# An encoder block on one core: selection for block 1 apart from that for blocks 2 and 3, a longer lead of A over V, and all gate rows made by ACT

## The chip, the core and the metric

The kernel runs on one core of a Trainium2 chip. TensorE (PE) multiplies matrices, VectorE (DVE) and ScalarE (ACT) do element-wise work, GpSimd (POOL) does element-wise work and issues indirect DMAs, SyncE (SP) issues plain DMAs. Each engine works through its own instructions strictly in the order in which they were issued and waits on semaphores for the others; so an instruction that waits holds up all that stand behind it on its engine. DMA transfers share 16 DMA engines.

The metric is the device time of one launch in microseconds (us). Three runs of the kernel before took 3649.86, 3670.61 and 3675.56 us; the median is 3670.61 us. In this kernel a difference below about 1% (some 37 us) can't be told from no change.

## What is computed

One layer of an encoder, on 512 tokens of width 2048, in float32: RMS norm, one input projection, attention and a short convolution, their gated sum through `w_out`, then PEER, then a small gated embedding. The change lies in PEER:

```python
q = (xc @ w_q).reshape(PEER_CHUNK, PEER_HEADS, 2, PEER_HALF)      # 8 heads, two halves of 128
s = jnp.einsum('thpc,hpnc->thpn', q, sub_keys)                    # 128 keys for each half
sv, si = lax.top_k(s, 16)                                         # the best 16 of each half
cand = sv[:, :, 0, :, None] + sv[:, :, 1, None, :]                # 16 x 16 sums
tv, tpos = lax.top_k(cand, 16)                                    # the best 16 of them
gate = jax.nn.softmax(tv, axis=-1)
a = jnp.einsum('td,thkd->thk', xc, u[eidx])                       # eidx: one of 16384 experts
hid = jax.nn.gelu(a) * gate
out = jnp.einsum('thk,thkd->td', hid, v[eidx])
```

Each token thus picks 8 x 16 = 128 experts of 16384; `u` and `v` have a row of 2048 numbers for each expert.

## The kernel before

The 512 tokens are four blocks of 128. The program is written in the order in which each engine is to work (a schedule by hand): Python generators hand over after a stretch of work, and credits in nominal microseconds set how much of one strand is issued between two pieces of another. Most weights are split into a high and a low part (ACT makes the high part, DVE or POOL the low one), and a product takes three matmuls (`mm3`, lines 218 to 220).

PEER is done in two ways. For **blocks 0 and 1** the picked rows are fetched: an indirect DMA, issued by POOL (`gather`, line 390), brings one row of `u` or `v` for each of the 128 tokens, 1.05 MB, and one DVE instruction over 128x2048 uses it (line 417 for `u`, line 440 for `v`, which adds to `gp`). Each block takes 128 such steps for `u` and 128 for `v`. They are a background strand `bg`: `bg(us)`, called at many places in the program, adds credit, and a step is issued while credit is positive (a step costs 2.45 of credit). The constants that begin with BG are the credits of the places. Four buffers `rows` hold fetched rows; a gather waits on POOL until DVE has used the row before in its buffer.

For **blocks 2 and 3** (256 tokens) all 16384 experts are multiplied, in 128 chunks of 128. `A` (line 1226 and following: `split_u`, and the matmuls) makes `a = u h` for a chunk, 48 matmuls over 256 columns, with gelu on ACT at line 1368. `V` multiplies the gated result with `v`; one `v_step` is 12 matmuls over 512 columns and a sum on DVE (`add_up`, line 1279), two steps for a chunk. The gates come from a dense matrix G (token by expert), which is built from the picks: `one_hots` makes, for four tokens at a time, rows `oj` (a one where the second index is) and `oi` (the gate's value where the first index is); four matmuls multiply them (`Gp`, line 1184), ACT evicts (`Gst`, line 1185), and the result goes to DRAM. There are 64 such groups.

The order of the part that matters here:

- **The queries** (`peer_q`, called at the end with blocks 1 to 3): for each of 8 heads the query matmuls `qA` (block 1) and `qB` (blocks 2, 3) in four pieces, with `bg(BG2)` after each; then `scores` makes the scores `hp`, and `sel.head` selects the best 16 on DVE. `Sel(3)` does this for three blocks in one go. With more than one block, `head` lets ACT spread the positions into `eq` (line 567) between two pieces of DVE work.
- **A alone**: `A` for the first LA chunks, with no `V`. Beside it runs `prepare` (what is left of the selection, then the 64 groups of G), BGD of credit to each quarter of a chunk, and `bg` with BG0. For chunks 0 to LA-9 the gelu goes to DRAM (`gad`) and is fetched again later.
- **V catches up**: at chunk LA, 2 x (LA - 8) steps of `V` alone, with `bg(BGV)` after each.
- **A and V together** for the chunks LA to 127, `V` 8 chunks behind, with `bg(BGU)` four times a chunk.
- Then the last 8 chunks of `V`, what is left of `bg`, and the embedding.

In `one_hots`, the first NACT of the four `oi` rows of a group are made by ACT (Abs of the difference, then Relu), row number NACT by POOL, the others by DVE.

Of the kernel before, what the change touches and what calls it, by code (L numbers as in the profile page):

```python
# [9 lines left out]
F32 = mybir.dt.float32  # L10
# [4 lines left out]
AF = mybir.ActivationFunctionType  # L15
# [3 lines left out]
P = 128  # L19
# [15 lines left out]
PH = 8  # L35
TOPK = 16
# [7 lines left out]
WSR = 8  # L44
BGA = 1.0
BGE = 0
LA = 24
BGV = 1.5
WSP = 8
WS0 = 4  # L50
BGF = 1.6
EV0 = 2
BG0 = 1.2
BGU = 1.5
BG1 = 2.2
BG2 = 1.5
BGD = 1.7
STEP = 2.45
VB = 7
WSH = 8  # L60
LAGC = 8
AHEAD = 3
NACT = 1
NROWS = 4


# [1 line left out]
def block_kernel(ctx: ExitStack, tc: tile.TileContext, a, out):  # L68
    nc = tc.nc
    ctx.enter_context(tc.manual_schedule())  # L70

    def pool(name, bufs=1, **kw):
        return tc.tile_pool(name=name, bufs=bufs, **kw)
# [13 lines left out]
    def bank(name, group=None):  # L87

        group = group or every[0]
        i = banks_used[group] = banks_used.get(group, -1) + 1  # L90
        tag = group[i % len(group)]
        return (pp if tag in LOW else high[0]).tile([P, 512], F32, name=name, tag=tag, bufs=1)


    class Stream:
        def __init__(self):
            self.items, self.loaded, self.parts, self.halves = [], 0, [], []
            self.used, self.share, self.turn = 0, 0, 0
# [124 lines left out]
    ident = cp.tile([P, P], F32, name="ident")  # L223
# [84 lines left out]
    TB = 2 * P  # L308
    TR = S - P
    u_t, v_t = a["peer_u"][0], a["peer_v"][0]  # L310
    gd = dp.tile([16, P, P, 16], F32, name="gd")
    gad = dp.tile([LA - LAGC, P, TB], F32, name="gad")
    x1d = dp.tile([2, P, D], F32, name="x1d")
# [13 lines left out]
    def tmp(shape, dt=F32, nm="t1"):  # L327
        return lt.tile([P] + shape, dt, name=nm, tag="t1", bufs=tbufs[0])
# [185 lines left out]
    class Sel:  # L514
# [4 lines left out]

        def __init__(self, nb):  # L520
            self.nb = nb
            self.tv = lt.tile([P, nb, PH, TOPK], F32, name="tv", tag="tv")
            self.ij = [lt.tile([P, nb, P], F32, name=f"ij{s}", tag=f"ij{s}") for s in range(2)]
            self.gate = lt.tile([P, nb, P], F32, name="gate", tag="gate")

        def head(self, h, hp):
            nb, tv = self.nb, self.tv
# [49 lines left out]
        def finish(self):  # L577
# [9 lines left out]
            nc.vector.reciprocal(gs, gs)  # L587
            nc.vector.tensor_mul(gv, gv, gs[:, :, None].to_broadcast([P, nb * PH, TOPK]))

    def scores(h, psA, psB, sel, blk):  # L590
        qA = tmp([256], nm="qa")
        nc.scalar.activation(qA, psA[:, :256], AF.Copy)
        hp = lt.tile([P, sel.nb, 2, P], F32, name="hp", tag="hp", bufs=2)
        if psB:
            qB = lt.tile([P, 2, TB], F32, name="qb", tag="h2B", bufs=6)
            for s in range(2):
                nc.scalar.activation(qB[:, s, :], psB[s][:, :TB], AF.Copy)
        yield
        pt = bank("qt", ("b3",))
        for s in range(2):  # L600
            nc.tensor.transpose(pt[:, s * P:(s + 1) * P], qA[:, s * P:(s + 1) * P], ident)
        qt = tmp([256], nm="qt")
        nc.scalar.activation(qt, pt[:, :256], AF.Copy)
        if psB:
            pk = bank("ks", ("b3",))
            for b in range(2):
                for s in range(2):
                    i = b * 2 + s
                    nc.tensor.matmul(pk[:, i * P:(i + 1) * P], qB[:, s, b * P:(b + 1) * P], keysT[:, 2 * h + s, :],
                                     start=True, stop=True)  # L610
            nc.scalar.activation(hp[:, 1:].rearrange("p b s n -> p (b s n)"), pk, AF.Copy)
        yield
        pk = bank("ks", ("b3",))
        for s in range(2):
            nc.tensor.matmul(pk[:, s * P:(s + 1) * P], qt[:, s * P:(s + 1) * P], keysT[:, 2 * h + s, :],
                             start=True, stop=True)
        nc.scalar.activation(hp[:, 0].rearrange("p s n -> p (s n)"), pk[:, :256], AF.Copy)
        yield
        yield from sel.head(h, hp)
        hs = slice(h * TOPK, (h + 1) * TOPK)  # L620
        i, j = (x[:, 0, hs] for x in sel.ij)
        nc.vector.scalar_tensor_tensor(i, i, 128.0, j, op0=ALU.mult, op1=ALU.add)
        nc.vector.tensor_copy(idxA[blk][:, hs], i)
        bg.add(u_steps(blk, h))
# [38 lines left out]
    def finish_A(b, sel):  # L663
        sel.finish()
        nc.vector.tensor_copy(gateA[b], sel.gate[:, 0, :])
        bg.add(v_steps(b))
# [45 lines left out]
    with pool("p0", side="right") as p0:  # L712
# [65 lines left out]
        ps = bank("cw", LOW)  # L778
# [186 lines left out]
    lt = lta = lts.enter_context(pool("late0", side="right"))  # L965
# [14 lines left out]
    for p_ in range(8):  # L980
        r = {}
        for nm, x, kt in (("ga", h0, KC), ("gc", h0, KC), ("ya", attn0, 8), ("yc", conv0, 8)):
            ps = bank(nm)
# [27 lines left out]
    sel = Sel(1)  # L1011
# [50 lines left out]
    with pool("mix2") as m2:  # L1062
        for p_ in range(8):
            sg = {}
            for nm, xh, xl, kt in (("ga", hH, hL, KC), ("gc", hH, hL, KC), ("ya", attnH, attnL, 8),
# [11 lines left out]
                for n in range(2):  # L1077
                    ps = pss[n][:, :TR]
# [33 lines left out]
    for c in range(0, KC, 2):  # L1112
        for dst, t0 in ((mA, 0), (mB, P)):
            t = mrg[:, c:c + 2, t0:t0 + dst[0].shape[2]]
            h = dst[0][:, c:c + 2, :]
# [4 lines left out]
    lt = lts.enter_context(pool("late", side="right"))  # L1120
    nc.sync.dma_start(x1_1, xv[1])
    for b in range(2):
# [5 lines left out]
    tA, tB = tA_pair(), tB_pair()  # L1128
    rsA[1] = rs[:, 0:1]
    turn = turner([(accB[0], rs[:, 1:2], tB, 0), (accB[1], rs[:, 2:3], tB, 1), (x1_1, rs[:, 0:1], tA, 0)], gffn,  # L1130
                  lambda: lt.tile([P, 512], F32, name="h2B", tag="h2B", bufs=6))
    for q in range(1, 4):
        turn(q)
    sel = Sel(3)
    ws.share = WSH
    sel_rest = peer_q(tA, tB, sel, 1, BG2)

# [4 lines left out]
    def prepare():  # L1142
        nonlocal dn
        yield from sel_rest
        finish_A(1, sel)
        yield 3.0
        for b in range(2):
            ps = bank("pkt", ("b2",))
            for i, t in enumerate((sel.ij[0], sel.ij[1], sel.gate)):
                nc.tensor.transpose(ps[:, i * P:(i + 1) * P], t[:, 1 + b, :], ident)  # L1150
            for i in range(3):
                nc.scalar.activation(pickT[i][:, b * P:(b + 1) * P], ps[:, i * P:(i + 1) * P], AF.Copy)
        nc.scalar.mul(pickT[3], pickT[0], -1.0)
        lts.close()
        dn = dns.enter_context(pool("dense"))
        yield 1.0
        def one_hots(t0):
            oj = dn.tile([P, 4, P], F32, name="oj", tag="vraw", bufs=4)
            oi = dn.tile([P, 4, P], F32, name="oi", tag="vh" if t0 % 8 else "vl", bufs=VB)

            for i in range(NACT):
                nc.scalar.activation(oi[:, i, :], io128, AF.Abs, bias=pickT[3][:, t0 + i:t0 + i + 1])
            for i in range(NACT):
                nc.scalar.activation(oi[:, i, :], oi[:, i, :], AF.Relu, bias=pickT[2][:, t0 + i:t0 + i + 1],
                                     scale=-4.0)
            nc.vector.tensor_tensor(oj, pickT[1][:, t0:t0 + 4, None].to_broadcast([P, 4, P]),
                                    io128[:, None, :].to_broadcast([P, 4, P]), op=ALU.is_equal)
            for i in range(NACT, 4):
                t = slice(t0 + i, t0 + i + 1)
                (nc.gpsimd if i == NACT else nc.vector).tensor_scalar(  # L1170
                    oi[:, i, :], io128, pickT[0][:, t], pickT[2][:, t], op0=ALU.is_equal, op1=ALU.mult)
            return oj, oi

        nxt = [one_hots(4 * i) for i in range(3)]
        for tg in range(16):
            st = dn.tile([P, P, 16], F32, name="Gst", tag="G", bufs=2)
            for q in range(4):
                t0 = tg * 16 + q * 4
                oj, oi = nxt.pop(0)
                if t0 + 12 < TB:  # L1180
                    nxt.append(one_hots(t0 + 12))
                ps = bank("Gp", ("b2", "b3"))
                for i in range(4):
                    nc.tensor.matmul(ps[:, i * P:(i + 1) * P], oj[:, i, :], oi[:, i, :], start=True, stop=True)
                nc.scalar.activation(st[:, :, q * 4:q * 4 + 4].rearrange("p i t -> p t i"),
                                     ps.rearrange("p (t i) -> p t i", t=4), AF.Copy)
                yield 1.3
            nc.scalar.dma_start(gd[tg], st)

    dn = None  # L1190
# [31 lines left out]
    def split_u(c, q):  # L1222
# [3 lines left out]
        nc.scalar.activation(h, t, AF.Copy)  # L1226
        (nc.gpsimd if q == 3 or (c < LA and q == 1) else nc.vector).tensor_sub(l, t, h.bitcast(F32))  # L1227
        uq[c, q] = (h, l)
# [71 lines left out]
    only = [False]  # L1300
    SP = LA - LAG

# [20 lines left out]
    for c in range(NCH + LAG):  # L1323
        if c + 1 < NCH:
            load_u(c + 1)
        if c < NCH:
            pa = bank("a", ("b0", "b1"))[:, :TB]
        if c == LA - 5:
            for _ in prep:
                pass  # L1330
            for i in range(4):
                load_ga(i)
        if c == LA - 4:
            load_G(0)
        if c == LA - 3:
            load_G(1)
# [17 lines left out]
        for q in range(4):  # L1354
# [4 lines left out]
            if c < LA:  # L1359
                dve += BGD  # L1360
                while dve > 0:
                    dve -= next(prep, 100.0)
            if q % 2 == 1 and c >= LA:
                v_step(2 * (c - LAG) + q // 2)
            bg((BG0 if c < LA - 5 else BG0 / 3) if c < LA else BGU if c < NCH else BGV / 2)
        if c < NCH:
            t = ring[:, c % 9, :]
# [141 lines left out]
```

## Time and profile before

| | |
|---|---|
| median of three runs | 3670.61 us |
| the profiled execution | 3676.39 us |
| its span, first to last instruction | 3674.6 us |
| mean granted clock of TensorE | 0.959 |
| busy PE / DVE / POOL / ACT | 90% / 73% / 59% / 41% |
| DMA moved | 1131.94 MB, mean 308 GB/s |

The profile is of one execution, by the hardware. A row of the timeline has its start and length in us, the engine, the line, the operation and what it writes and reads; `x3` says that three like it follow each other, with one length for all. A row of groups has busy time, the mean of one in ns, and the idle time before them with what ended it. A row of the windows has one stretch. PE's busy time is no measure of PE at its peak, since matmuls overlap.

### The profile page before, as it was taken

Reading aid. Unit: us, or ns where it says so; the run is one execution under the profiler, and the core shown is the slowest. Engines: PE = TensorE matmul, PEld = TensorE weight load, DVE = VectorE, ACT = ScalarE, POOL = GpSimd, SP = SyncE. Lnnn points to the kernel's source line nnn. Section 1 sums busy time; section 2 is a strip of 40 time slices with the busy share of each in tenths; the row PEclk is TensorE's granted clock in tenths of the full one; section 3 lists DMA queues with packets and bytes.
Section 4 is the critical chain, followed back from the end, with each engine's and each line's share of the span. In section 5 each row is a group of like instructions: output and inputs, shape, how many; then the busy total and the mean of one; then the engine's idle time right before and its main releaser. Section 6 shows DMA issues by size and latency. Waiting matters only on the chain. (4 is left out here: it accounts for less than half of the span.)

```text
span 3674.6 us, 53569 instructions
## 1 busy us (share of the span) xinstructions
PE 3295.4 (90%) x19455; PEld 2955.6 (80%) x19455; DVE 2697.4 (73%) x3844; ACT 1507.9 (41%) x2822; POOL 2166.2 (59%) x1764
## 2 busy tenths in 40 slices
PE   7999888999999998777787898999998999899899
PEld 5999677889999977767775777888887888788687
DVE  7458688776555655999978897887887988977411
ACT  5258523343333333327743333444433443334422
POOL 2012046567888776436754676777777777776343
PEclk8999999999999999988999999999999999999899
DMA  5689778888999997548898999999999999997332
GB/s 208 219 314 339 261 274 293 295 293 337 357 356 347 366 346 269 185 162 293 314 362 317 333 380 358 396 363 392 379 361 364 378 384 384 370 374 273 126 120 81
DMA packets 265501, 1131.94 MB, mean 308 GB/s; under 512 B 25980, under 2 KB 64148, under 8 KB 195092
## 3 DMA queue, kind: packets, MB, share of 16 engines
q1 hardware_dynamic: 186324, 568.54, 43.5%
q0 software_dynamic: 74304, 541.10, 38.3%
q10 hardware_dynamic: 4608, 18.88, 1.3%
q8 instruction: 153, 2.51, 0.3%
q14 instruction: 112, 0.92, 0.1%
HBM read 1102.20 MB, written 26.21 MB: 307 GB/s over the span
## 5 line engine op out<-in xcount | busy, mean ns | idle before, releaser
L131 POOL TENSOR_TENSOR wl<-wraw,wh 128x512 fp32r<-128x512 f32 x534 | 694.7, 1308 | 544.3 <-ACT wh L129 532.5
L1213 POOL TENSOR_TENSOR vl<-vraw,vh 128x512 fp32r<-128x512 f32 x464 | 610.1, 1336 | 375.4 <-ACT vh L1212 318.0
L129 ACT ACTIVATE wh<-wraw 128x512 fp32r<-128x512 f32 x696 | 430.2, 630 | 685.1 <-PE gt L220 117.4
L440 DVE SCALAR_TENSOR_TENSOR gp<-rows,dots,gp 128x2048 f32<-128x2048 f32 x254 | 596.6, 2349 | 109.3 <-DMA rows<-in_peer_v_dram,idx 108.8
L417 DVE SCALAR_TENSOR_TENSOR rows<-rows,gp 128x2048 f32<-128x2048 f32 x256 | 581.9, 2280 | 113.5 <-DMA rows<-in_peer_u_dram,idx 113.5
L220 PE MATMUL a<-tBH,ul 128*128 128x256 f32 x2048 | 583.1, 285 | 11.4 <-DVE ul L1227 11.4
L218 PE MATMUL a<-tBH,uh 128*128 128x256 f32 x2048 | 587.0, 287 | 6.1 <-ACT uh L1226 6.1
L219 PE MATMUL a<-tBL,uh 128*128 128x256 f32 x2048 | 581.6, 284 | 0.0
L218 PE MATMUL o<-vh,hidH 128*128 128x512 f32 x1024 | 425.2, 415 | 156.2 <-DVE accB L1279 149.3
L1227 DVE TENSOR_TENSOR ul<-uraw,uh 128x512 fp32r<-128x512 f32 x360 | 415.5, 1161 | 172.5 <-ACT uh L1226 170.2
L1226 ACT ACTIVATE uh<-uraw 128x512 fp32r<-128x512 f32 x512 | 311.4, 627 | 544.0 <-PE a L219 266.4
L219 PE MATMUL o<-vl,hidH 128*128 128x512 f32 x1024 | 417.4, 408 | 3.7 <-POOL vl L1213 3.7
L220 PE MATMUL o<-vh,hidL 128*128 128x512 f32 x1024 | 415.7, 406 | 0.0
L218 PEld LDWEIGHTS a<-tBH,uh 128*128 128x128 f32 x2048 | 394.7, 193 | 15.7 <-ACT uh L1226 7.1
L220 PEld LDWEIGHTS a<-tBH,ul 128*128 128x128 f32 x2048 | 393.7, 192 | 13.3 <-DVE ul L1227 13.2
L219 PEld LDWEIGHTS a<-tBL,uh 128*128 128x128 f32 x2048 | 393.7, 192 | 8.8
L218 PEld LDWEIGHTS o<-vh,hidH 128*128 128x128 f32 x1024 | 200.3, 196 | 217.2 <-DVE accB L1279 150.9
L390 POOL DMA_INDIRECT rows<-in_peer_v_dram,idx x256 | 278.3, 1087 | 98.6 <-DVE gp L440 44.6
L1212 ACT ACTIVATE vh<-vraw 128x512 fp32r<-128x512 f32 x512 | 295.0, 617 | 90.2 <-PE o L220 87.2
L390 POOL DMA_INDIRECT rows<-in_peer_u_dram,idx x256 | 271.2, 1060 | 100.6 <-DVE rows L417 49.2
L1227 POOL TENSOR_TENSOR ul<-uraw,uh 128x512 fp32r<-128x512 f32 x152 | 201.1, 1323 | 89.8 <-ACT uh L1226 84.6
L219 PEld LDWEIGHTS o<-vl,hidH 128*128 128x128 f32 x1024 | 201.1, 196 | 46.9 <-POOL vl L1213 11.0
(388 smaller groups left out, 7103.0 us busy)
## 6 DMA issues: line engine op xcount, KB each, us to landing
uraw<-in_peer_u_cols_dram SPq DMA_DIRECT2D x256, 512.0 KB, 10.2
vraw<-in_peer_v_tiles_dram SPq DMA_DIRECT2D x256, 512.0 KB, 7.5
wraw<-in_w_in_gates_dram SPq DMA_DIRECT2D x96, 512.0 KB, 6.4
wraw<-in_w_in_conv_dram SPq DMA_DIRECT2D x64, 512.0 KB, 5.1
wraw<-in_w_out_dram SPq DMA_DIRECT2D x64, 512.0 KB, 5.6
wraw<-in_w_peer_q_dram SPq DMA_DIRECT2D x64, 512.0 KB, 4.6
wraw<-in_w_in_qkv_dram SPq DMA_DIRECT2D x40, 512.0 KB, 4.7
wring<-in_w_in_conv_dram SPq DMA_DIRECT2D x32, 512.0 KB, 4.6
```

The costliest lines, as they stand in the source:

```text
L129: nc.scalar.activation(h, t, AF.Copy)
L131: (nc.gpsimd if self.turn >= 8 else nc.vector).tensor_sub(l, t, h.bitcast(F32))
L218: nc.tensor.matmul(ps, ah, bh, start=first, stop=False)
L219: nc.tensor.matmul(ps, ah, bl, start=False, stop=False)
L220: nc.tensor.matmul(ps, al, bh, start=False, stop=last)
L390: nc.gpsimd.indirect_dma_start(out=dst, out_offset=None, in_=src, in_offset=bass.IndirectOffsetOnAxis(ap=ix, axis=0))
L417: nc.vector.scalar_tensor_tensor(t[0], t[0], 1.0, gp[0], op0=ALU.mult, op1=ALU.mult, accum_out=dots[b][:, k:k + 1])
L440: nc.vector.scalar_tensor_tensor(gp[0], t[0], dots[b][:, k:k + 1], gp[0], op0=ALU.mult, op1=ALU.add)
L1212: nc.scalar.activation(h, t[:, i, :], AF.Copy)
L1213: (nc.vector if only[0] and i else nc.gpsimd).tensor_sub(l, t[:, i, :], h.bitcast(F32))
L1226: nc.scalar.activation(h, t, AF.Copy)
L1227: (nc.gpsimd if q == 3 or (c < LA and q == 1) else nc.vector).tensor_sub(l, t, h.bitcast(F32))
```

## The change

Four things change, and the credits with them.

1. `peer_q` for blocks 1 to 3 now selects for block 1 alone (`sel = Sel(1)`). The scores of blocks 2 and 3 are kept in tiles `hpB`, one for each head, and a second object `selB = Sel(2)` selects from them in `prepare`, after the first selection has ended, beside A.
2. LA goes from 24 to 48. So A runs alone for 48 chunks, `gad` holds 40 chunks in place of 16, and V catches up with 80 steps in place of 32.
3. NACT goes from 1 to 4: ACT makes all four `oi` rows of a group, POOL and DVE none.
4. BG2 goes from 1.5 to 5.0 (queries), BG0 from 1.2 to 0.85 and BGD from 1.7 to 0.93 (A alone), and a group of G counts 0.8 in place of 1.3.

```diff
-LA = 24
+LA = 48
-BG0 = 1.2
+BG0 = 0.85
-BG2 = 1.5
-BGD = 1.7
+BG2 = 5.0
+BGD = 0.93
-NACT = 1
+NACT = 4
@@ scores
-        hp = lt.tile([P, sel.nb, 2, P], F32, name="hp", tag="hp", bufs=2)
+        hp = lt.tile([P, 1, 2, P], F32, name="hp", tag="hp", bufs=2)
         if psB:
-            qB = lt.tile([P, 2, TB], F32, name="qb", tag="h2B", bufs=6)
+            qB = lt.tile([P, 2, TB], F32, name="qb", tag="h2B", bufs=HB)
+            hpB[h] = lt.tile([P, 2, 2, P], F32, name="hpB", tag="h2B", bufs=HB)
...
-            nc.scalar.activation(hp[:, 1:].rearrange("p b s n -> p (b s n)"), pk, AF.Copy)
+            nc.scalar.activation(hpB[h].rearrange("p b s n -> p (b s n)"), pk, AF.Copy)
@@ the main stage
-    sel = Sel(3)
+    sel, selB = Sel(1), Sel(2)
@@ prepare
         yield from sel_rest
         finish_A(1, sel)
+        yield 1.5
+        for h in range(PH):
+            for _ in selB.head(h, hpB[h]):
+                yield 2.5
+        selB.finish()
         yield 3.0
         for b in range(2):
             ps = bank("pkt", ("b2",))
-            for i, t in enumerate((sel.ij[0], sel.ij[1], sel.gate)):
-                nc.tensor.transpose(ps[:, i * P:(i + 1) * P], t[:, 1 + b, :], ident)
+            for i, t in enumerate((selB.ij[0], selB.ij[1], selB.gate)):
+                nc.tensor.transpose(ps[:, i * P:(i + 1) * P], t[:, b, :], ident)
@@ one_hots
-                (nc.gpsimd if i == NACT else nc.vector).tensor_scalar(
+                nc.vector.tensor_scalar(
@@ G
-                yield 1.3
+                yield 0.8
```

How the change moves instructions can be read from the built programs. The first place is DVE in the queries, one head of the selection. Before, with `gp<-rows` a background step, the best-16 rows come by threes (three blocks):

```order
L440 SCALAR_TENSOR_TENSOR gp<-rows,dots_93,gp 128x2048
L546 TENSOR_TENSOR cand<-sv 128x3x48
L546 TENSOR_TENSOR cand<-sv 128x3x52
L549 CAST sif<-si 128x96
L504 MAX tv<-cand 128x8 x3
L506 MAX_INDEX tp<-tv,cand 128x8 x3
L508 MATCH_REPLACE z_13602<-tv,cand 128x100 x3
```

and of the change, at the same place:

```order
L440 SCALAR_TENSOR_TENSOR gp<-rows,dots_93,gp 128x2048 x2
L546 TENSOR_TENSOR cand<-sv 128x48
L546 TENSOR_TENSOR cand<-sv 128x52
L549 CAST sif<-si 128x32
L504 MAX tv<-cand 128x8
L506 MAX_INDEX tp<-tv,cand 128x8
L508 MATCH_REPLACE z_13891<-tv,cand 128x100
L510 MAX tv<-z_13891 128x8
L512 MAX_INDEX tp<-tv,z_13891 128x8
L440 SCALAR_TENSOR_TENSOR gp<-rows,dots_93,gp 128x2048 x3
```

One block in place of three is selected, and more background steps stand between. From the last `tAL` (the transposed input of the queries) to the first `ul` (A's first split on DVE) there are 65 background steps now and 20 before.

The second place is DVE beside A, in the changed program, where the low parts `ul` of A's weights (line 1235 there) now alternate with the selection from `hpB`; before, one-hot rows stood here from chunk 3 on:

```order
L440 SCALAR_TENSOR_TENSOR gp<-rows,dots_93,gp 128x2048
L1235 TENSOR_TENSOR ul<-uraw,uh 128x512
L504 MAX sv<-hpB 128x8 x2
L506 MAX_INDEX si<-sv,hpB 128x8 x2
L508 MATCH_REPLACE z<-sv,hpB 128x128 x2
L510 MAX sv<-z 128x8 x2
L512 MAX_INDEX si<-sv,z 128x8 x2
```

Counted by `ul` (two to a chunk), the selection from `hpB` lies in the chunks 3 to 29, the 64 `oj` rows in the chunks 30 to 43 (before: 3 to 14). There are 38 background steps in the chunks 0 to 29. Where A and V run together, the last background step stands in chunk 110 (before: in chunk 126), 2.45 a chunk in both programs.

The third place is ACT in the groups of G, before (`uh`: the high part of A's weights, `ring`: gelu):

```order
L1162 ACTIVATE oi<-io_86,picks 128x128
L1164 ACTIVATE oi<-oi,picks 128x128
L1185 ACTIVATE Gst<-Gp 128x4x128
L1368 ACTIVATE ring<-a 128x256
L1370 DMA gad<-ring 128x256
L1226 ACTIVATE uh<-uraw 128x512
```

and of the change:

```order
L1376 ACTIVATE ring<-a 128x256
L1378 DMA gad<-ring 128x256
L1234 ACTIVATE uh<-uraw 128x512
L1170 ACTIVATE oi<-io_86,picks 128x128 x4
L1172 ACTIVATE oi<-oi,picks 128x128 x4
L1193 ACTIVATE Gst<-Gp 128x4x128
```

A group has eight rows for `oi` on ACT in place of two.

## Rows read from the trace of the kernel before

**Rows 1.** Windows: busy us (instructions) of each engine, granted clock, DMA share, GB/s
```profile
core 0: us, PE busy (x) PEld busy (x) DVE busy (x) ACT busy (x) POOL busy (x), PEclk, DMA share, GB/s
1436.30:1638.60 202.30, 162.28 (x1264) 160.07 (x1263) 173.85 (x646) 66.06 (x123) 98.69 (x82) 0.91 0.55 185
1638.60:1693.00 54.40, 36.48 (x207) 34.59 (x207) 49.72 (x134) 25.75 (x50) 21.48 (x21) 0.68 0.53 170
1693.00:1845.00 152.00, 122.95 (x970) 117.38 (x970) 150.01 (x207) 120.77 (x226) 115.80 (x101) 0.97 0.92 336
1845.00:1921.30 76.30, 66.11 (x499) 63.58 (x498) 52.29 (x41) 31.35 (x59) 39.89 (x33) 0.94 1.01 378
1921.30:2066.00 144.70, 108.63 (x409) 82.38 (x410) 114.90 (x141) 48.18 (x95) 66.32 (x55) 0.89 0.88 317
2066.00:3388.30 1322.30, 1203.17 (x7460) 1072.21 (x7459) 1124.35 (x1099) 535.81 (x1043) 951.25 (x764) 0.97 0.96 369
3500.00:3600.00 100.00, 100.00 (x430) 80.26 (x429) 11.74 (x16) 27.60 (x45) 47.53 (x36) 1.00 0.37 116
```

**Rows 2.** Waits, 1430 to 1640: who for whom, total us, times, longest
```profile
PE ks L609 <- ACT qt L603: 39.3, 8, 10.3
ACT eq L567 <- DVE ab L558: 35.4, 7, 7.6
```

**Rows 3.** Groups of instructions on DVE in the queries, 1436.3 to 1638.6
```profile
L440 DVE SCALAR_TENSOR_TENSOR gp<-rows,dots,gp 128x2048 f32<-128x2048 f32 x20 | 46.9, 2344 | 3.3 <-DMA rows<-in_peer_v_dram,idx 3.2
L504 DVE MAX8 sv<-hp 128x8 f32<-128x128 f32 x42 | 9.4, 279 | 19.4 <-ACT hp L617 19.4
```

**Rows 4.** Timeline of DVE, block 0's selection: first instruction of two heads
```profile
452.42 0.48 DVE L504 MAX8 sv<-hp 128x8 f32<-128x128 f32 x2
460.55 0.48 DVE L504 MAX8 sv<-hp 128x8 f32<-128x128 f32 x2
```

**Rows 5.** Groups of instructions on DVE while A runs alone, 1640 to 1921
```profile
L1227 DVE TENSOR_TENSOR ul<-uraw,uh 128x512 fp32r<-128x512 f32 x47 | 41.0, 873 | 27.7 <-ACT uh L1226 27.7
```

**Rows 6.** Groups of instructions on ACT while A runs alone, 1640 to 1921
```profile
L1226 ACT ACTIVATE uh<-uraw 128x512 fp32r<-128x512 f32 x97 | 59.3, 628 | 61.5 <-DMA uraw<-in_peer_u_cols_dram 36.2 <-PE a L219 14.7 <-PE a L220 2.6
L1164 ACT ACTIVATE oi<-oi,picks 128x128 f32<-128x128 f32 x64 | 25.7, 402 | 2.1
```

**Rows 7.** Timeline of ACT beside A
```profile
1674.81 0.59 ACT L1152 ACTIVATE picks<-pkt 128x128 f32<-128x128 f32 x3
...
1709.70 0.40 ACT L1164 ACTIVATE oi<-oi,picks 128x128 f32<-128x128 f32 x1
1710.01 1.04 ACT L1185 ACTIVATE Gst<-Gp 128x512 f32<-128x512 f32 x1
1710.86 0.63 ACT L1226 ACTIVATE uh<-uraw 128x512 fp32r<-128x512 f32 x1
...
1715.15 0.41 ACT L1368 ACTIVATE ring<-a 128x256 f32<-128x256 f32 x1
1716.05 0.63 ACT L1226 ACTIVATE uh<-uraw 128x512 fp32r<-128x512 f32 x1 [0.48 <-DVE gp L440]
```

**Rows 8.** Timeline of DVE beside A: two gate rows of a group
```profile
1710.35 0.60 DVE L1170 TENSOR_SCALAR oi<-io,picks 128x128 f32<-128x128 f32 x2
```

**Rows 9.** Timeline of DVE: first and thirty-first sum of V's catch-up steps
```profile
1934.49 0.68 DVE L1279 TENSOR_TENSOR accB<-o,accB 128x512 f32<-128x512 f32 x1
...
2060.71 0.68 DVE L1279 TENSOR_TENSOR accB<-o,accB 128x512 f32<-128x512 f32 x1
```

**Rows 10.** Timeline of ACT: gelu of two chunks in succession, A and V together
```profile
2236.86 0.36 ACT L1368 ACTIVATE ring<-a 128x256 f32<-128x256 f32 x1
2248.03 0.36 ACT L1368 ACTIVATE ring<-a 128x256 f32<-128x256 f32 x1
```

**Rows 11.** Groups of instructions on PE while A runs alone, 1640 to 1921
```profile
L1184 PE MATMUL Gp<-oi,oj 128*128 128x128 f32 x512 | 75.1, 290 | 31.0 <-DVE oi L1170 12.3 <-DVE oj L1166 10.5 <-ACT Gst L1185 3.4
```

More of the change, by code (lines that the diff above doesn't have):

```diff
@@ L521, in __init__ @@
             self.nb = nb
-            self.tv = lt.tile([P, nb, PH, TOPK], F32, name="tv", tag="tv")
-            self.ij = [lt.tile([P, nb, P], F32, name=f"ij{s}", tag=f"ij{s}") for s in range(2)]
-            self.gate = lt.tile([P, nb, P], F32, name="gate", tag="gate")
+            self.tv = lt.tile([P, nb, PH, TOPK], F32, name="tv", tag=f"tv{nb}")
+            self.ij = [lt.tile([P, nb, P], F32, name=f"ij{s}", tag=f"ij{s}{nb}") for s in range(2)]
+            self.gate = lt.tile([P, nb, P], F32, name="gate", tag=f"gate{nb}")
         def head(self, h, hp):
@@ L588, in finish @@
             nc.vector.tensor_mul(gv, gv, gs[:, :, None].to_broadcast([P, nb * PH, TOPK]))
+    HB, hpB = 10, {}
     def scores(h, psA, psB, sel, blk):
@@ L1130, in block_kernel @@
     turn = turner([(accB[0], rs[:, 1:2], tB, 0), (accB[1], rs[:, 2:3], tB, 1), (x1_1, rs[:, 0:1], tA, 0)], gffn,
-                  lambda: lt.tile([P, 512], F32, name="h2B", tag="h2B", bufs=6))
+                  lambda: lt.tile([P, 512], F32, name="h2B", tag="h2B", bufs=HB))
     for q in range(1, 4):
         turn(q)
-    sel = Sel(3)
+    sel, selB = Sel(1), Sel(2)
     ws.share = WSH
```

## The prediction

> **What bounds the kernel now.** I read the windows first, cut at the borders of the stages, because the stages have different limits [rows 1]. The queries (1436.3 to 1638.6) have DVE busy for 173.9 of 202.3 us and DMA at a share of only 0.55. While A runs alone (1638.6 to 1921.3, three rows, 282.7 us) the middle row, in which the groups of G are made, has DVE busy for 150.0 of 152 us: DVE is the bound there. In the row after it G is done, and DMA is the bound, at a share of 1.01 and 378 GB/s. V's catch-up (144.7 us) has no full engine. In the long stretch with A and V together (1322.3 us for 104 chunks, 12.71 each) PE is busy for 91%, DVE for 85%, and DMA runs at 0.96: all near their limit.
>
> The waits then tell why the queries take 202 us although DVE is not full: ACT waits 35.4 us for the positions that it is to spread, and PE waits 39.3 us for ACT behind that [rows 2].
>
> The change spends on one side and earns on another: 24 chunks leave the long stretch, and 24 chunks of A alone and 48 steps of V alone take their place; the groups of G move from three engines to one. So I sum up five terms, in the order of the program.
>
> **Queries.** There are 65 background steps here in place of 20. At 2.344 us [rows 3] they are 152 us of DVE. The 42 first maxima of [rows 3] are 7 heads of the selection for three blocks (6 each), and 173.9 less 46.9 for the 20 steps and some 7 for the transposed inputs leaves 120, or 17.1 us a head. A head for one block takes 460.55 - 452.42 = 8.1 us [rows 4]; 7 of them are 57 us. With the 7 this makes 216 us for DVE. DMA: 185 GB/s over 202.3 us is 37.4 MB [rows 1]; 45 more rows of 1.05 MB make 84.6 MB, at 378 GB/s 224 us. ACT's wait for the positions goes, since one block has no such step, but POOL's gathers still wait for DVE's buffers, and PE's weights are split on POOL behind them. I take 230 us, **+28**; bounds 216 (+14) and 250 (+48, both limits imperfectly overlapped).
>
> **A alone, chunks 0 to 29.** No row has a selection for two blocks; I take the middle between 8.1 and 17.1, 12.6 us a head, and the two ends as bounds. Eight heads are 101 us; 38 background steps at 2.344 are 89; 60 low parts at 873 ns [rows 5] are 52; what is left of the first selection, the two softmaxes and the steps between two blocks some 23. The sum is 265 us, and at DVE's 99% of the middle row [rows 1] 268; I say 270, 9.0 a chunk. PE's own work for such a chunk is less: V's matmuls take 100 / 430 = 0.233 us each [rows 1], 24 of them 5.58, and two chunks in succession of A and V together have been 11.17 us apart [rows 10]; so A's part is 5.59. Bounds: 235 with the selection at 8.1, 322 with 17.1 and low parts at twice the price.
>
> **A alone, chunks 30 to 43.** All 64 groups of G fall here, 4.6 to a chunk. DVE has only little left (an `oj`, two low parts, 1.4 steps: about 8 us a chunk). But each group has eight rows on ACT. From the start of a Relu to the start of what follows it is 1710.01 - 1709.70 = 0.31 us, and from the eviction to the next start 0.85 [rows 7]. So a group is 8 x 0.31 + 0.85 = 3.33 us, and 64 are 213. To each of the 14 chunks come four high parts of 0.63 [rows 6] and 0.90 for gelu and its transfer, from 1715.15 to 1716.05 [rows 7]: 48 in all. Sum 261; I take 260 us, 18.6 a chunk, against 12.7 for such a chunk before (152 us for 12). ACT becomes the bound here, with nothing to cover it: A's own high parts stand in the same queue. Bounds: with three evictions in 0.59 us [rows 7], 0.20 apiece, 64 x 2.42 + 48 = 203; with the whole 0.402 [rows 6] and 1.06, 64 x 4.28 + 48 = 322.
>
> The Trainium skill has a price for a run of such rows: on "ScalarE: Activation LUTs" (section "What ACT_TABLE_LOAD costs") an ACTIVATE with a bias by pointer takes some 280 ns and 0.833 ns an element, less 93 ns of overlap. By it, an estimate from that page, a row of 128 would be 0.294 us and the term 253 us; the 0.402 of [rows 6] is near its 387 ns without overlap, and no row before has four in succession. The same page (section "Rules for kernel authors") would give Relu and multiplication to VectorE, which speaks against this part. The trace agrees: DVE made two gate rows in 0.60 us [rows 8], ACT needs two instructions for each.
>
> **A alone, chunks 44 to 47.** Nothing stands beside A; nine such chunks took 76.3 us [rows 1], so four are 34. A alone is then 270 + 260 + 34 = 564 us, **+281** to 282.7.
>
> **V catches up.** Sums of 30 steps lie between 1934.49 and 2060.71, 4.21 us a step [rows 9]; the window of 144.7 us, less 13 until the first sum, gives 4.1 for 32. PE's own 12 matmuls take 2.79, but only two banks take V's results, and their sums on DVE stand behind background steps. The work to a step stays as it was, so 48 more are 48 x 4.1 = **+197** (bounds 134 at PE's own pace, and 202).
>
> **A and V together.** 80 chunks in place of 104. The last background step stands in chunk 110, so 63 chunks have as many as before and take 12.71, and 17 have none, and run at PE's pace, 11.2 [rows 10]. That is 801 + 190 = 991, **-331**. Bounds: all 80 at 12.71 (-305); the 63 at 12.5 (-345).
>
> **Sum.** +28 + 281 + 197 - 331 = +175 us. The profiled execution took 3676.4 us, 5.8 over the median; 3851 against it is **3845 us** against the median of 3670.6. Slower by 4.8%.
>
> **Rivals.** (a) *V alone runs at PE's pace.* If its sums no longer come late, 80 steps take 13 + 223 = 236 us in place of 342, and the time is 3740. For it: the transfers for V run at a share of 0.88 only. Against it: DVE keeps the same steps, and was busy for 115 of 145 us [rows 1].
>
> (b) *ACT packs the gate rows at 0.20 us.* The term is 203, the time 3788. Against it: 0.31 after a Relu. With (a) too, 3682: no change.
>
> (c) *Faster: A alone goes at PE's pace.* The place is the 48 chunks, the mechanism that splits, selection and gate rows run far enough ahead of PE that only matmuls count: 48 x 5.59 and 75 for G [rows 11] are 343 us, 221 less than my 564, and the time is 3624. It decides from about 390 us for the stretch, where the sum is zero. For it: POOL has nothing to do with G now, and DVE has less. Against it: the sum of DVE's work in chunks 0 to 29 alone is 265, and ACT's in the next 14 at least 203, and these two can't overlap, since G needs the finished selection.
>
> (d) *The clock.* Where PE waits much, the granted clock was 0.68 [rows 1]. At that, A's 5.59 becomes 8.2, still below 9.0, and costs nothing. Only at 1.2 GHz throughout would PE be the bound: 30 x 11.2 and 14 x (11.2 + 10.7) are 643 in place of 530, and the time 3958.
>
> **How the numbers follow.** My forecast has a chance of 0.57, (a) 0.12, (b) 0.11, (a) with (b) 0.06, (c) 0.08, (d) 0.06. The range leaves out (c), the two together and (d): it goes from 3720, below (a), to 3920, where the upper bounds of the selection (+52) and part of that of the gate rows lie. Since a difference of 1% (37 us) is about what can be told from no change, (c) is the chance of faster, 0.08; (a) with (b) is that of no change, 0.06; the others, 0.86, are slower.
>
> **What would show it.** In the profile after: the queries near 230 us with DVE almost full and DMA above 350 GB/s; gelu of a chunk every 9 us in chunks 0 to 29 and every 18 or 19 us in chunks 30 to 43, there with ACT nearly always busy and POOL idle for half of the time; sums in V's catch-up about 4.1 us apart for some 340 us; then 12.7 us a chunk until the background ends, and 11.2 in the last 17. The forecast is wrong if the stretch of A alone is under 450 us, or if V's catch-up is under 270.

## The result

The changed kernel takes 3858.64 us (median of four runs, 3846.18 to 3868.26) beside 3673.09 us for the kernel before. The ratio on record is 1.0545, with a 95% interval from 1.0511 to 1.0579; the quotient of these two medians alone is 1.0505. So the change costs between 186 us (by the medians) and 199 us (by the ratio). The kernel before had lower medians, from 3654.89 to 3664.22 us, beside the experiments, so kernels that ran at different times are compared by their ratios. The forecast was 3845 us, 4.8% slower, with a range from 3720 to 3920.

| | before | after |
|---|---|---|
| the profiled execution | 3676.39 us | 3859.42 us |
| its span | 3674.6 us | 3857.6 us |
| mean granted clock of TensorE | 0.959 | 0.945 |
| busy PE / DVE / POOL / ACT | 90% / 73% / 59% / 41% | 87% / 69% / 53% / 42% |
| DMA moved | 1131.94 MB, mean 308 GB/s | 1138.28 MB, mean 295 GB/s |

The windows of the profile after are cut at the same events as those of before [rows 1]: the queries; A alone in chunks 0 to 29, 30 to 43 and 44 to 47; V's catch-up; A and V together while background steps last, and without them. The columns are the same.

```profile
core 0: us, PE busy (x) PEld busy (x) DVE busy (x) ACT busy (x) POOL busy (x), PEclk, DMA share, GB/s
1434.50:1662.20 227.70, 171.43 (x1263) 165.11 (x1264) 210.79 (x339) 55.78 (x109) 137.39 (x125) 0.92 0.92 355
1662.20:1967.10 304.90, 218.37 (x1489) 208.77 (x1487) 274.50 (x733) 113.95 (x223) 131.16 (x107) 0.85 0.80 284
1967.10:2206.90 239.80, 172.07 (x1151) 162.50 (x1152) 99.53 (x124) 229.13 (x615) 53.07 (x45) 0.85 0.62 215
2206.90:2238.10 31.20, 25.41 (x188) 24.77 (x186) 14.33 (x14) 12.53 (x25) 14.72 (x11) 0.89 0.92 322
2238.10:2575.00 336.90, 255.91 (x958) 194.67 (x959) 269.02 (x346) 109.55 (x206) 163.54 (x130) 0.91 0.87 309
2586.20:3385.40 799.20, 722.33 (x4480) 643.08 (x4478) 682.78 (x614) 323.02 (x631) 571.39 (x459) 0.97 0.97 370
3385.40:3573.00 187.60, 187.60 (x1212) 170.27 (x1211) 75.47 (x118) 87.67 (x168) 110.77 (x86) 1.00 0.57 185
```

What to see: the bound changes from row to row. DVE is busy for 93% of the queries with DMA at a share of 0.92, and for 90% of chunks 0 to 29. In chunks 30 to 43 it is ACT, for 229.1 of 239.8 us, while DVE and POOL rest. At the end PE is full for 187.6 us.

To put it against the forecast, the stages run from the first matmul of the queries over the first of A to gelu of chunk LA-1, of chunk LA, and of chunk 127:

| stage | before | after | difference | forecast |
|---|---|---|---|---|
| queries | 202.7 | 227.7 | +25.0 | +28 |
| A alone | 282.7 | 575.9 | +293.2 | +281 |
| V's catch-up, to gelu of chunk LA | 151.9 | 348.1 | +196.2 | +197 |
| A and V together, to gelu of chunk 127 | 1315.2 | 986.8 | -328.4 | -331 |
| sum | | | +186.0 | +175 |

The spans differ by 183.0 us, so hardly anything is outside these four.

Three more views of after. The waits in the queries: where before PE waited for ACT behind the positions [rows 2], it now waits for the low parts of its weights, which stand on POOL behind gathers that wait for DVE.

```profile
POOL rows L390 <- DVE gp L440: 71.3, 23, 5.3
...
PE qA L219 <- POOL wl L131: 51.2, 20, 4.9
```

The timeline of ACT in the groups of G, which answers to [rows 7]: four Abs, four Relu, the eviction, and the next group.

```profile
2041.44 1.31 ACT L1170 ACTIVATE oi<-io,picks 128x128 f32<-128x128 f32 x4
2042.66 1.26 ACT L1172 ACTIVATE oi<-oi,picks 128x128 f32<-128x128 f32 x4
2043.83 1.03 ACT L1193 ACTIVATE Gst<-Gp 128x512 f32<-128x512 f32 x1
2044.67 1.23 ACT L1170 ACTIVATE oi<-io,picks 128x128 f32<-128x128 f32 x4
```

From the first Relu to the eviction four rows take 2043.83 - 2042.66 = 1.17 us, 0.29 each, and a group 2044.67 - 2041.44 = 3.23 us. The groups of DVE there show who waits:

```profile
L1235 DVE TENSOR_TENSOR ul<-uraw,uh 128x512 fp32r<-128x512 f32 x28 | 19.4, 692 | 147.0 <-ACT uh L1234 147.0
```

DVE stands idle for 147.0 us before its 28 low parts, each time for the high part, which stands in ACT's queue between two groups.

### The profile page after: what moved, and what is told of

It reads as the page before. It is cut to its first block, busy times and chain, and to the rows that moved or that the text cites. A ratio compares the mean times of both kernels' runs of the same rounds, so it can differ in the third digit from the quotient of the medians.

```text
span 3857.6 us, 54167 instructions
## 1 busy us (share of the span) xinstructions
PE 3355.6 (87%) x19455; PEld 3002.6 (78%) x19455; DVE 2668.6 (69%) x3872; ACT 1616.5 (42%) x3209; POOL 2060.2 (53%) x1676
## 2 busy tenths in 40 slices
DMA packets 272419, 1138.28 MB, mean 295 GB/s; under 512 B 26748, under 2 KB 71060, under 8 KB 202004
## 5 line engine op out<-in xcount | busy, mean ns | idle before, releaser
L1221 POOL TENSOR_TENSOR vl<-vraw,vh 128x512 fp32r<-128x512 f32 x416 | 549.9, 1341 | 408.7 <-ACT vh L1220 327.2
L220 PE MATMUL a<-tBH,ul 128*128 128x256 f32 x2048 | 598.9, 292 | 71.9 <-DVE ul L1235 69.5
L218 PE MATMUL a<-tBH,uh 128*128 128x256 f32 x2048 | 601.0, 293 | 11.4 <-ACT uh L1234 11.4
L1235 DVE TENSOR_TENSOR ul<-uraw,uh 128x512 fp32r<-128x512 f32 x336 | 340.2, 1019 | 370.5 <-ACT uh L1234 369.3
L219 PE MATMUL a<-tBL,uh 128*128 128x256 f32 x2048 | 593.9, 290 | 0.0
L220 PEld LDWEIGHTS a<-tBH,ul 128*128 128x128 f32 x2048 | 407.0, 199 | 79.9 <-DVE ul L1235 76.9
L218 PEld LDWEIGHTS a<-tBH,uh 128*128 128x128 f32 x2048 | 409.0, 200 | 19.0 <-ACT uh L1234 12.5
L219 PEld LDWEIGHTS a<-tBL,uh 128*128 128x128 f32 x2048 | 407.7, 199 | 6.7
L1235 POOL TENSOR_TENSOR ul<-uraw,uh 128x512 fp32r<-128x512 f32 x176 | 234.0, 1331 | 313.8 <-ACT uh L1234 303.8
L220 PEld LDWEIGHTS o<-vh,hidL 128*128 128x128 f32 x1024 | 201.5, 197 | 45.9 <-DVE hidL L1256 0.2
```

Of the source, the lines that this page charges most:

```text
L218: nc.tensor.matmul(ps, ah, bh, start=first, stop=False)
L219: nc.tensor.matmul(ps, ah, bl, start=False, stop=False)
L220: nc.tensor.matmul(ps, al, bh, start=False, stop=last)
L1221: (nc.vector if only[0] and i else nc.gpsimd).tensor_sub(l, t[:, i, :], h.bitcast(F32))
```

## The experiments

All compute the whole result. Ratios are against the kernel before, run beside on the same chip, with 95% intervals.

### 1. The gate rows shared out again

```diff
-NACT = 4
+NACT = 1
...
-                nc.vector.tensor_scalar(
+                (nc.gpsimd if i == NACT else nc.vector).tensor_scalar(
```

> The changed kernel with the gate rows shared out again as before (one of four by ACT, one by POOL, two by DVE). Theory: eight rows a group on ACT set the pace of chunks 30 to 43, 239.8 us. With two rows ACT has 64 x (0.73 + 0.85) + 48 = 149 us there, and DVE 64 x 1.3 + 14 x (3.2 + 1.7) = 152, so the stretch falls to 150 to 170 us and the whole to about 3780 us. Rival: PE (at a granted clock of 0.85 there) or the chain from row to eviction sets the pace; then the stretch stays over 215 us and the whole over 3835.

Measured: 3776.31 us, 1.0314 (1.0265 to 1.0363), in place of 1.0545. The windows, chunks 30 to 43:

```profile
1959.30:2114.80 155.50, 143.94 (x1178) 140.43 (x1177) 146.79 (x246) 135.70 (x254) 120.52 (x107) 0.98 0.90 326
```

The stretch falls from 239.8 to 155.5 us, and the profiled span by 85.5. All other stages stay within 5 us. PE, DVE and DMA are at 90 to 94% now, ACT at 87%, and PE's granted clock is back at 0.98 from 0.85. So the three more rows of each group that the change gave to ACT cost some 84 us of the 186, and the theory's number (150 to 170) was right.

### 2. The longer lead alone

```diff
-LA = 24
+LA = 48
```

(in the kernel before)

> The kernel before with a lead of 48 in place of 24, nothing else. Theory: chunks of A alone beside nothing take about 8.2 us (DMA full), a step of V alone 4.1, a chunk of both together 12.7: 24 x 8.2 + 48 x 4.1 - 24 x 12.7 = +89, and some 77 background steps that are made earlier leave about 31 chunks at 11.2 (-47): +42, 3715 us. Rival 1: the lead is the main loss of the change: over +100, 3775 or more. Rival 2: nothing is lost by it: within 15 us of before.

Measured: 3749.19 us, 1.0253 (1.0212 to 1.0294), +91 us between the medians, with +62 between the two profiled executions (that of the kernel before took 3676.39 us, 18 over the median beside this experiment, and that of this kernel 10 less than its own). By stage, in those: A alone 458.7 us (+176.0, 7.3 for each of 24 more chunks), catch-up 350.5 (+198.6), both together 1005.4 (-309.8). The chunks of A beside nothing run at DMA's pace, as expected: the window of 32 of them shows 8.0 us each.

```profile
1821.00:2077.00 256.00, 209.67 (x1534) 191.86 (x1534) 194.87 (x166) 88.94 (x172) 144.65 (x123) 0.96 1.01 403
```

My use of the credit was wrong: 77 more steps are made before the long stretch, as I had counted, but the 24 chunks that leave it would have made 59 themselves, so only 18 steps, some 7 chunks, are saved at its end. The last step stands at chunk 118 and not at 97. That turns the -47 into about -10, and +42 into +79. So the +91 lies between the theory (+42) and rival 1 (over +100), and nearer to the rival: the longer lead by itself costs 2.5%.

### 3. The selection for blocks 2 and 3 alone beside A

The kernel before with `Sel(1)` in the queries, `Sel(2)` in `prepare`, as in the diff of the change, and the lead of 24; and

```diff
-BGD = 1.7
+BGD = 2.75
```

> The kernel before with the selection of blocks 2 and 3 taken out of the queries and put beside A (lead 24 as before, the credit BGD at 2.75 so that it fits into 19 chunks). Theory: the queries fall from 202 to about 150 us, since DVE has 47 + 57 + 7 = 111 us there and PE sets the pace; beside A, DVE gets some 105 us more, and A alone goes from 283 to about 385. Net +50, 3723 us. Rival 1: the selection beside A costs no more than it saves in the queries: within 20 us of before. Rival 2: its waits cost far more: over 3770.

Measured: 3702.00 us, 1.0119 (1.0079 to 1.0158). The windows of the queries and of A alone:

```profile
1429.40:1585.70 156.30, 151.26 (x1264) 149.15 (x1265) 118.24 (x310) 55.72 (x109) 98.81 (x81) 1.00 0.70 240
1585.70:1950.60 364.90, 250.15 (x1673) 233.41 (x1671) 319.33 (x849) 182.72 (x348) 180.69 (x154) 0.82 0.69 246
```

The queries fall to 156.3 us, PE's pace (151.3 us busy, clock 1.00), and A alone rises to 364.9: -46.4 and +82.2, where the theory had about -52 and +102. DVE is the engine that both share: beside A it gets 67 us more, and not the 105 of the theory (319.3 in place of 49.7 + 150.0 + 52.3 = 252.0 [rows 1]), and in the queries 118.2 us are left to it.

### 4. The queries with as little background as before

```diff
-BG2 = 5.0
+BG2 = 1.5
```

(in the changed kernel)

> The changed kernel with the background credit in the queries back at 1.5 (20 background steps there in place of 65). Theory: DVE and DMA set the pace of the queries, 227.7 us; with 45 steps fewer they fall to about 150 us, PE's pace; the 45 steps fill the last 17 chunks again, at 12.7 in place of 11.2 us: +26. Net -52, 3807 us. Rival: PE and its weights set the pace of the queries: they stay over 200 us, and the whole is 3858 or more.

Measured: 3802.13 us, 1.0390 (1.0349 to 1.0431), against 1.0545: -1.5%, about -55 us. The queries in the windows:

```profile
1441.00:1597.20 156.20, 151.16 (x1265) 149.06 (x1265) 118.28 (x311) 55.73 (x109) 98.62 (x81) 1.00 0.70 240
```

227.7 falls to 156.2 us (-71.5), so the 45 background steps cost 1.6 us each there. They cost more behind it: A alone takes 556.4 in place of 575.9 us (-19.5), nearly all of it in chunks 0 to 29, which take 286.9 in place of 304.9:

```profile
1597.20:1884.10 286.90, 217.79 (x1489) 207.03 (x1487) 263.01 (x675) 110.51 (x215) 131.76 (x104) 0.87 0.79 281
```

In the changed kernel DVE comes to A's first low part only at 1671.2 us, 8.9 us after PE's first matmul of A, since work of the queries still stands before it; here it comes to it at 1596.6, before that matmul. With this the 45 steps cost 91 us, 2.0 each. Later they cost less: the long stretch takes 1011.5 in place of 986.9 us, and the time from there to the end 11 us more, 36 us together or 0.8 a step. The difference, 55 us, is near that of the medians, 56. So the change had put the steps where they are dear: the 65 steps in the queries filled DVE and DMA, while the chunks that they would have filled ran at PE's pace.

### 5. Four banks for V alone

```diff
-        ps = bank("o", ("b2", "b3"))
+        ps = bank("o", LOW if alone[0] else ("b2", "b3"))
...
+            alone[0] = True
             for n in range(2 * SP):
                 v_step(n)
                 bg(BGV)
+            alone[0] = False
+            add_up()
```

(in the changed kernel; `LOW` are four banks, the two of A among them, and the line that takes A's bank is moved behind this, so that V can have them)

> The changed kernel with four PSUM banks in place of two for V's results while V runs alone (A's two banks are free there). Theory: V alone takes 4.12 us a step and not 2.79 since, with two banks, PE waits for DVE's sums (73.8 us of waits over 78 steps); with four a late sum is made up, and the step falls to DVE's own pace, about 3.4 us: -55, 3803 us. Rival: DVE's order of work sets the pace whatever the banks: the step stays over 3.95 us, and the whole over 3845.

Measured: 3839.84 us, 1.0488 (1.0455 to 1.0521) against 1.0545: -0.5%, some 20 us, with intervals that touch; 26 us in the catch-up (322.0 in place of 348.1). PE's idle time in its groups there has another cause now:

```profile
L219 PE MATMUL o<-vl,hidH 128*128 128x512 f32 x317 | 135.5, 428 | 40.5 <-POOL vl L1221 26.0 <-DVE vl L1221 14.0
L218 PE MATMUL o<-vh,hidH 128*128 128x512 f32 x316 | 128.8, 408 | 6.3 <-ACT vh L1220 6.3
```

From the sum of step 1 to that of step 78 a step takes 3.82 us in place of 4.17 (the 4.12 of the expectation divides the same 321 us by 78 and not by 77). The 73.8 us of waits for sums are gone, but V's low parts, made by POOL and DVE, come late in their place (40.0 us of waits), so that less than half of the expected 55 us came. DVE is busy for 271 of 315 us there.

### 6. V alone without background

```diff
                 v_step(n)
-                bg(BGV)
```

(in the changed kernel, in the catch-up)

> The changed kernel without background steps while V runs alone (49 steps move to the end of the background). Theory: the 2.3 us background steps ahead of the sums on DVE make V alone slow: the step falls from 4.12 to about 3.0 us (-90); 42 of the steps fill the last 17 chunks (+26), the others come behind: net -55, 3803 us. Rival: splits of V's weights and the hidden values set the pace: the step stays over 3.8 us, and the whole over 3855.

Measured: 3825.70 us, 1.0449 (1.0417 to 1.0481). The catch-up:

```profile
2238.00:2505.00 267.00, 237.62 (x963) 185.69 (x962) 158.18 (x242) 108.06 (x202) 117.65 (x81) 0.96 0.63 200
```

A step falls to 3.34 us, where 3.0 was expected, and the catch-up to 282.3 us (-65.8, for an expected -90); the long stretch takes 20.1 us and the time behind it 14.4 us more, where the 49 steps now are. What is left, some 33 us, is little more than half of the -55. So background work on DVE is the greater part of what V alone waits for, as the theory said, but even without it a step is 0.55 us over PE's 2.79: the sums still make PE wait for 29.4 us in the waits of this kernel.

### 7. The positions spread by DVE

```diff
-            if nb > 1:
+            if nb > 3:
                 for s, eq in enumerate(eqs):
                     nc.scalar.activation(eq, wide[s], AF.Copy)
```

(in the changed kernel)

> The changed kernel with the positions of the selection for blocks 2 and 3 spread by DVE itself and not by ACT. Chunks 0 to 29 took 305 us where 270 was forecast, with DVE busy for 274.5. Theory: ACT waits there for the positions (38.8 us in 8 waits), A's high parts stand behind that, and DVE then waits for them; without it the stretch falls to 280 to 290 us: -15 to -25, some 3838 us. Rival: the 30 us are not from that, and DVE's dearer comparison adds 5 us: 3859 to 3865.

Measured: 3862.32 us, 1.0552 (1.0517 to 1.0587), no difference from the change. A head has one stretch of work less for the credit, so the groups of G come some chunks earlier, and the stretch has to be compared as a whole. Of A alone, all 48 chunks, first in the changed kernel

```profile
1662.20:2238.10 575.90, 415.85 (x2825) 396.04 (x2823) 388.37 (x871) 355.61 (x860) 198.95 (x163) 0.85 0.73 257
```

and then in this one:

```profile
1651.90:2234.70 582.80, 414.44 (x2825) 393.70 (x2823) 394.84 (x875) 346.75 (x846) 197.11 (x163) 0.86 0.73 255
```

DVE has 6.5 us more work, the stretch 6.9 us more. So taking away ACT's waits for the positions gains nothing over A alone, where 15 to 25 us had been expected; the rival was right. Chunks 0 to 29 by themselves can't be compared, since groups of G stand in them here.

### 8. Both repairs in the kernel before

The edits of experiments 7 and 5 in the kernel before.

> The kernel before with two edits: positions spread by DVE itself in the selection for three blocks, and four banks for V alone. Theory: in the queries PE waits 39.3 us for ACT behind the positions; without it they fall from 202 to about 182 us (DVE's own work); V's 32 steps alone fall by 0.6 us each: -20 and -19, 3633 us. Rival: DVE sets the pace in both places, and gets some 5 us more: 3670 to 3680.

Measured: 3672.50 us, 1.0023 (1.0005 to 1.0041): not faster. The windows of the queries and of A alone tell why:

```profile
1439.40:1622.70 183.30, 158.76 (x1265) 155.52 (x1265) 161.49 (x577) 55.85 (x109) 99.65 (x80) 0.93 0.58 199
1622.70:1921.30 298.60, 228.79 (x1672) 219.78 (x1671) 274.35 (x452) 177.20 (x330) 178.76 (x155) 0.87 0.83 302
```

The queries fall to 183.3 us, just as forecast, since PE no longer waits behind the positions (3.4 us there in place of 39.3). But DVE had not finished its part, and A alone takes 298.6 in place of 282.7. The two together are 481.9 us, and were 485.4, with DVE busy for 435.8 us of them, where it was for 425.9: what the queries gain, A alone gives back. That DVE sets the pace of the two is read from this. The catch-up gains 6.9 us, where 19 were expected, and the long stretch gives 4.9 back. The rival's time (3670 to 3680) came.

### 9 and 10. A little of the background moved ahead

The kernel before with the four banks, and for the two runs

```diff
-BG1 = 2.2
+BG1 = 2.35
-BGU = 1.5
+BGU = 1.46
```

or 2.5 and 1.42.

> The kernel before with four banks for V alone, and with some background steps moved from the long stretch (BGU 1.46 in place of 1.5) to the stages ahead of the queries (BG1 2.35 in place of 2.2; 7 steps more before A). Theory: between 800 and 1270 us PE is full and DMA at 0.93, so these steps cost nothing there, and each saves 0.8 to 2.7 us in the long stretch, where DMA is at 0.96: -6 to -19; the four banks -7: 3640 to 3650 us. Rival: the weights come late in the earlier stages and it is given back: within 5 us of before.

> The same with twice as much moved (BG1 2.5, BGU 1.42; 15 steps more before A). Theory: -12 to -40 in the long stretch and -7 from the banks: 3620 to 3645 us. Rival: DMA, at 0.93 to 0.95 ahead of the queries, has no room for 15 MB more in some 615 us, PE waits for weights there, and the time is at or over that of before.

Measured: 3643.87 us, 0.9965 (0.9940 to 0.9990), and 3644.98 us, 0.9967 (0.9945 to 0.9989), against 3654.89 beside them. Both are 0.3% faster than the kernel before, with intervals that end just under 1, and equal to each other. Between 800 and 1270 us DMA went up and PE stayed full; the stretch of before is

```profile
800.00:1270.00 470.00, 466.19 (x2673) 463.85 (x2671) 285.82 (x252) 163.57 (x274) 386.28 (x322) 1.00 0.93 350
```

and that of run 9:

```profile
800.00:1270.00 470.00, 466.20 (x2670) 463.54 (x2668) 304.60 (x256) 163.53 (x275) 391.46 (x329) 1.00 0.95 362
```

So the steps that moved ahead were hidden there: the queries begin at 1437.2 and 1437.1 us, and did at 1435.9. The long stretch takes 1292.9 and 1291.0 us in place of 1315.2. These stages overstate the gain, since the profiled execution of the kernel before was a long one: by the medians it is 11 and 10 us. For the first run that is just short of the 13 to 26 expected, and for the second well short of the 19 to 47, though both times lie within the times that were named, which counted from a slower kernel before. Why the second run gained no more than the first isn't settled, and how the gain divides between the banks and the moved steps wasn't tried apart.

## Why the prediction was right

The sum came within 11 us (+186.0 for +175), but part of that is luck: two terms of A alone missed by 35 us one way and by 20 us the other.

**Queries** (+28; measured +25.0). The step held: DVE has 210.8 us of work of the 216 that were summed up, DMA moves at 355 GB/s. Experiment 4 shows the cause from the other side: with 20 background steps PE sets the pace, at 156 us. What the term left out is that the queries' work on DVE doesn't end with them: three of the 65 steps ran beside A.

**Chunks 0 to 29** (270; measured 304.9). This is the term that was mis-sized most, by 35 us. The work was right: DVE was busy for 274.5 us, and 42 background steps fell in the window where 38 were counted (three of them left over from the queries), so without four at 2.34 it is 265, the sum of the forecast. What failed is the step "at DVE's 99% of the middle row [rows 1] 268": DVE was busy for 90%, and idle for 30.4 us. The timeline shows where. The last 7.5 us are no more than the border: ACT's first row for G starts at 1957.0, 10 us before gelu of chunk 29, and DVE then waits for the next high part behind it. Another 8.1 us are one wait:

```profile
1712.03 0.63 ACT L337 ACTIVATE junk<-x 128x512 bf16<-128x512 f32 x1 [6.90 <-DVE x L452]
...
1721.26 0.63 ACT L1234 ACTIVATE uh<-uraw 128x512 fp32r<-128x512 f32 x1 [5.46 <-DMA uraw<-in_peer_u_cols_dram]
...
1721.92 0.69 DVE L1235 TENSOR_TENSOR ul<-uraw,uh 128x512 fp32r<-128x512 f32 x1 [8.13 <-ACT uh L1234]
```

ACT waits first for DVE's last work on block 1 (`x`), then for the weights `uraw`, and DVE waits for ACT. Some 10 us are six waits of 1.2 to 2.1 us, the rest short gaps. The waits of this stretch suggest a ring for the six:

```profile
PE a L220 <- DVE ul L1235: 69.5, 30, 8.8
...
ACT eq L567 <- DVE ab L558: 38.8, 8, 6.4
DVE ul L1235 <- ACT uh L1234: 18.4, 8, 8.1
```

PE waits for DVE's low parts up to 8.8 us at a time, since a piece of the selection stands ahead of them; ACT makes the next high parts only when PE has used the last ones; and DVE, done with its piece, then waits for those. This ring is read from the waits and was not changed by itself; experiment 7 shows that taking the positions away from ACT gains nothing. Experiment 4 shows that the load of the queries is a large part of it: without the 45 steps the same chunks take 286.9 us, 18 less, and DVE's longest wait for a high part is 2.6 us. The upper bound of the term, 322, doesn't come out of its own terms: with 17.1 us a head and low parts at twice the price the sum is 353.

**Chunks 30 to 43** (260; measured 239.8). ACT became the bound, as forecast, and experiment 1 shows it. The price of a row was 0.29 us and not 0.31, and the rows of four of the 64 groups had been made before, in the 10 us that the last term had too much. Here the price on the page "ScalarE: Activation LUTs" of the Trainium skill was the nearer one (an estimate of 0.294 by its section "What ACT_TABLE_LOAD costs"; 1.17 us for four in the timeline after). The rule of the same page of the Trainium skill that gives Relu and multiplications to VectorE (section "Rules for kernel authors") agrees with experiment 1, which gives three of four rows back to DVE and POOL and wins 84 us. The four chunks that follow took 31.2 us for 34.

**V's catch-up** (+197; measured +196.2). Sums of steps 1 and 78 lie between 2249.09 and 2570.02 us, 4.17 a step:

```profile
2249.09 0.68 DVE L1287 TENSOR_TENSOR accB<-o,accB 128x512 f32<-128x512 f32 x1
...
2570.02 1.27 DVE L1287 TENSOR_TENSOR accB<-o,accB 128x512 f32<-128x512 f32 x2
```

The reason given (two banks, and sums behind background steps) is borne out in both halves: experiment 5 takes away the first and wins 26 us, experiment 6 the second and wins 66 us there. The two were not taken away together.

**A and V together** (-331; measured -328.4). The last background step came in chunk 110. Before it a chunk takes 12.9 us (799.2 for 62), where 12.71 was counted, after it gelu to gelu is 3405.64 - 3394.47 = 11.17, as forecast:

```profile
3394.47 0.36 ACT L1376 ACTIVATE ring<-a 128x256 f32<-128x256 f32 x1
3405.64 0.37 ACT L1376 ACTIVATE ring<-a 128x256 f32<-128x256 f32 x1
```

**The rivals.** (a) is excluded: a step of V alone was 4.17 us, and 3.34 even without background. (b): 0.20 a row was not to be had. (c): A alone took 575.9 us, far over the 390 from which it would have decided, and DVE's and ACT's work did follow each other. (d): the granted clock was 0.85 there, and in chunks 30 to 43 ACT was busy for 96%, so PE's clock cost nothing that ACT had not taken already. Of the signs that were named, two came out otherwise in size: gelu came every 10.2 us in chunks 0 to 29 and every 17.1 in chunks 30 to 43.

Taken by themselves in the kernel before, the longer lead costs 91 us, the selection 44, and the gate rows, taken out of the changed kernel, 84. The sum of 219 is near the 186 to 199 that the whole change costs, but it leaves out the credits, the fourth part of the change: experiment 4 puts BG2 alone at 56 us. With it the sum is 275, so the parts do not simply add up. The lead and the selection were tried in the kernel before, the gate rows and BG2 within the change; how they overlap wasn't tried, nor the gate rows alone in the kernel before.

## What to carry to other kernels

Where two strands of matmuls run together near the limit of DMA, DVE and PE at once, running them one after the other costs time on both sides: each alone has its own bound (here DMA or DVE for A, the sums on DVE for V), and 24 chunks that in the long stretch of before took 12.7 us each took 7.3 (A) and 8.3 (V) apart (experiment 2: 176.0 and 198.6 over 24). Work that is moved should be counted on the engine that sets the pace where it arrives, by instructions and not by elements: on ACT a row of 128 is 0.39 us long and one of 512 (`uh`) 0.63, and eight small rows for each group made a side engine the bound at once. And the same background step cost 2.0 us in a stage with a full DVE (what it left to the next stage counted in) and 0.8 in one with room, so the place decides more than the amount.

## What the runs showed of the hardware

In the chunks of A alone of experiment 2, with rows fetched beside plain loads, DMA held 403 GB/s over 256 us at a share of 1.01; the highest row of [rows 1] had 378 at the same share, and the page of the kernel before shows 396 in one of its slices of 92 us. So 378, by which the forecast reckoned the queries, was no ceiling; that the mix of transfers makes the difference wasn't tried apart. And ACT's rows of 128 follow each other 0.29 us apart when four of a kind stand together, 0.1 us less than each is long.
